# RWKV preparation of a hybrid encoder block: gate tiles between its projections, low-rank products of 128 rows

## The chip, the cores and the metric

One core of one Trainium2 chip. The metric is the device time of one execution in microseconds (us). TensorE (PE) has a granted clock, which the profile shows as a share of full speed; its two levels are 1.2 and 2.4 GHz.

## The reference, cut to what matters

One encoder block on 1024 tokens of width 1024. All branches read one input projection:

```
h    = rms_norm(x)                      # 1024 x 1024
proj = h @ w_in                         # columns: q k v | r k v (512 each) w,a (64+64) g (128) | gates 2 x 1024
attn = windowed attention of q, k, v (128-token blocks, +-128 tokens, sink)
zr   = proj[rwkv columns], shifted: zr + mu * (0.5 * (left + right neighbour) - zr)
w    = w0 + tanh(wl) @ w2 ;  a = sigmoid(a0 + al @ a2)     # low rank, 64 -> 512, for 2 directions
rw   = two RWKV-7 scans (forward, backward) over the tokens, plus a bonus term, normed, times g
gates = sigmoid(proj[gate columns])
x    = x + (gates[0] * (attn @ w_up_attn) + gates[1] * (rw @ w_up_rwkv)) @ w_out
# then a squared-ReLU MLP and a gated per-layer embedding
```

## The kernel before, in words

All large products are of fp32 data split into a high and a low part, and each product is three: high x high, low x high, high x low. A projection tile is 128 output columns by 512 tokens (one half of the tokens): 8 pieces of the contraction x 3 = 24 products of 128x512 in one PSUM buffer. PSUM buffers of these tiles ("mm") are two. A weight tile of 128 columns is loaded in two parts (`load_w`, line 193): DMA on SP's queue, a cast to the high part on ACT (line 187), the low part as a difference on POOL (line 188). There are two buffers of it (tag "w").

The program is written down in one order, and a tile scheduler places each instruction on its engine: by that order and readiness in its own model of time. On the chip each engine goes through its queue in order. Stretches written with `tc.high_priority(offset=-LOW)` come last whenever anything else is ready. `mmo` and `after` pin an order.

The stages that the change touches:

*Preparation* (lines 476 to 687). The two low-rank inputs z12 and z13 come first. Then for each of four pairs of heads p: the projections kz, rz and vz (two halves, 48 products each), each put through `shifted` (line 510): ACT copies the tile to "zr" (one buffer) and a scaled copy to "z", POOL adds the two neighbours ("sm"), DVE combines. vz's products are written with two hooks: after 8 of them the bonus sums of the pair before (`add_bonus`: rk split in two, products with a matrix of ones, line 569 and 570, eight transposes to "vt", line 583) and the split of this pair's squares, after 23 the norm sums. Then for both directions two low-rank products (`lora`, line 541): per half one product of 128 rows (line 547: high weights, high and low input above each other) and one of 64 rows (line 548: low weights, high input). ACT, DVE and POOL work the results into ra, bk, kd, rk, which go to DRAM. The buffer tag "gth" (two) is shared by the gates' outputs and by the second half's splits.

*Gate tiles* (`gates`, line 280): 16 tiles of columns m for each half h, tanh of the tile to DRAM. Half 0 is written as the generator `gates0`: 152 of its 384 products (`F0`) stand between p=3's low-rank products, the other 232 and the first two tiles of half 1 (48 products) stand behind the attention loop at the lowest priority, so that they fill in where PE has nothing else. The other 14 tiles of half 1 run beside the scan (`beside`), as before and after the change.

*Attention* (lines 805 to 882): 8 blocks n of 128 tokens; for both kv heads scores (line 839), row maximum on DVE, exponentials on ACT, transposes (line 860), products with V (line 868). In block 3 the scan's first low products are added, in block 5 the first inverse, 62 small DVE steps (line 749 and 752).

*Scan* (from line 1144): begins with `load_step` (line 1040: bkc, rac, UV) and `products` (line 1027, "gps", whose results are written where half 0 of the normed input lay).

The load of kT from DRAM (line 463) is issued on POOL's queue right behind the q/k/v stage, whose last transposes write kT_d.

## Time and profile before

| what | value |
|---|---|
| median of 3 runs | 1830.6 us (1830.04 to 1831.61) |
| profiled execution | 1829.44 us, span of its instructions 1827.7 us |
| PE busy | 1718.2 us (94% of the span), 11288 products |
| DVE, ACT, POOL busy | 1132.3, 879.1, 320.2 us |
| mean granted clock of PE | 0.977 |

"Busy" of PE is a sum over products whose ends are modelled and that overlap, so a busy PE is not one at its peak. A row of a timeline has the start, the duration, engine, line, operation, output<-input, shapes, count, and in brackets how long the engine stood idle before it and what released it.

### The profile page before, as it was taken

How to read it: one execution, taken by the hardware profiler on the slowest of the kernel's cores; microseconds unless marked ns; L12 is line 12 of the kernel's file. 1: busy time of each engine (PE TensorE's matmuls, PEld its weight loads, DVE VectorE, ACT ScalarE, POOL GpSimd, SP SyncE). 2: the span in 40 equal slices, each digit the busy share in tenths (PEclk: the TensorE clock that was granted, in tenths of full speed). 3: DMA queues.
4: the chain of work that ended last, by engine and by line, in shares of the span. 5: the costliest groups of instructions: out<-in, count | busy, mean ns of one | idle time of the engine just before them, and what ended most of it. 6: DMA issues, size and time to landing. Idle time of an engine off the chain costs nothing. (4 is left out here: it accounts for less than half of the span.)

```text
span 1827.7 us, 29641 instructions
## 1 busy us (share of the span) xinstructions
PE 1718.2 (94%) x11288; PEld 1376.0 (75%) x11288; DVE 1132.3 (62%) x1931; ACT 879.1 (48%) x1624; POOL 320.2 (18%) x265
## 2 busy tenths in 40 slices
PE   7999888999999898988889989999999999999998
PEld 7976666666677777766668867787887888888887
DVE  5646777745935656676464387666665877685442
ACT  5536666547754555456532255444444444554321
POOL 3454544532132121112132000000000000000000
PEclk9999999989999999999899989999999999999999
DMA  6362444674377474576565305544445974574111
GB/s 202 99 176 73 124 144 144 196 204 115 102 202 202 141 196 139 170 208 199 178 211 175 104 35 162 171 146 133 158 154 208 318 251 127 190 219 136 61 41 46
DMA packets 281998, 285.96 MB, mean 156 GB/s; under 512 B 49408, under 2 KB 195712, under 8 KB 281728
## 3 DMA queue, kind: packets, MB, share of 16 engines
q1 hardware_dynamic: 273600, 270.76, 48.1%
q0 software_dynamic: 7824, 12.59, 2.5%
q8 instruction: 89, 1.46, 0.3%
q10 hardware_dynamic: 432, 0.73, 0.1%
q14 instruction: 53, 0.43, 0.1%
HBM read 203.26 MB, written 80.74 MB: 155 GB/s over the span
## 5 line engine op out<-in xcount | busy, mean ns | idle before, releaser
L188 POOL TENSOR_TENSOR wlo<-wst,whi 128x512 fp32r<-128x512 f32 x100 | 149.5, 1507 | 318.7 <-ACT whi L187 263.3
L1688 PE MATMUL ff2ps<-th,sh 128*128 128x512 f32 x448 | 173.7, 390 | 2.9 <-ACT th L187 2.9
L1688 PE MATMUL ff2ps<-tl,sh 128*128 128x512 f32 x448 | 174.3, 389 | 0.0
L1688 PE MATMUL ff2ps<-th,sl 128*128 128x512 f32 x448 | 174.3, 389 | 0.0
L175 POOL TENSOR_TENSOR rstd<-ms,neghalf 128x1 f32<-128x1 f32 x24 | 13.2, 553 | 803.4 <-DVE ms L173 803.4
L187 ACT CAST sh<-sst 128x512 fp32r<-128x512 f32 x109 | 67.8, 622 | 116.3 <-PE ff2ps L1688 71.7
L188 DVE TENSOR_TENSOR sl<-sst,sh 128x512 fp32r<-128x512 f32 x109 | 75.1, 689 | 54.1 <-ACT sh L187 53.7
L1688 PEld LDWEIGHTS ff2ps<-th,sh 128*128 128x128 f32 x448 | 83.9, 188 | 21.1 <-ACT th L187 3.6
L1688 PEld LDWEIGHTS ff2ps<-tl,sh 128*128 128x128 f32 x448 | 84.1, 188 | 17.5 <-DVE tl L188 0.2
L1688 PEld LDWEIGHTS ff2ps<-th,sl 128*128 128x128 f32 x448 | 84.1, 188 | 17.5
L187 ACT CAST whi<-wst 128x512 fp32r<-128x512 f32 x100 | 60.7, 618 | 51.1 <-DMA wst<-in_w_in_dram 17.7
L187 ACT CAST w1h<-w1st 128x512 fp32r<-128x512 f32 x48 | 29.1, 614 | 104.4 <-DMA w1st<-in_w_ff_dram 102.9
L188 DVE TENSOR_TENSOR w1l<-w1st,w1h 128x512 fp32r<-128x512 f32 x48 | 32.7, 687 | 57.3 <-ACT w1h L187 57.3
L208 PE MATMUL gps<-rm,bkp 128*128 128x256 f32 x256 | 62.4, 386 | 1.5 <-DVE Z L752 1.0
L1034 DVE TENSOR_TENSOR gm<-gps,gmask 128x512 f32<-128x512 f32 x64 | 43.7, 685 | 29.9 <-PE gps L208 29.9
L218 PE MATMUL gmm<-hh,wlo 128*128 128x512 f32 x144 | 58.9, 409 | 0.0
L216 PE MATMUL gmm<-hl,whi 128*128 128x512 f32 x144 | 58.9, 409 | 0.0
L214 PE MATMUL gmm<-hh,whi 128*128 128x512 f32 x144 | 58.8, 408 | 0.0
L187 ACT CAST w1h<-ssum 128x512 fp32r<-128x512 f32 x64 | 39.4, 615 | 35.9 <-DVE ssum L1324 23.8
L208 PEld LDWEIGHTS gps<-rm,bkp 128*128 128x128 f32 x256 | 47.5, 190 | 11.0 <-issue 1.5
L1086 DVE COPY Wt<-wps 64x512 f32<-64x512 f32 x16 | 10.9, 679 | 71.5 <-PE wps L208 71.5
L226 PE MATMUL mm<-hh,whi 128*128 128x512 f32 x128 | 51.4, 401 | 4.0 <-ACT z L520 4.0
(409 smaller groups left out, 5058.0 us busy)
## 6 DMA issues: line engine op xcount, KB each, us to landing
wst<-in_w_in_dram SPq DMA_DIRECT2D x92, 256.0 KB, 3.5
tst<-in_w_ff_dram SPq DMA_DIRECT2D x80, 256.0 KB, 3.9
w1st<-in_w_ff_dram SPq DMA_DIRECT2D x32, 512.0 KB, 5.5
hid_S<-h SPq DMA_DIRECT2D x64, 256.0 KB, 2.1
sst<-hid_S SPq DMA_DIRECT2D x64, 256.0 KB, 2.7
hid_A<-h SPq DMA_DIRECT2D x48, 256.0 KB, 2.0
sst<-hid_A SPq DMA_DIRECT2D x45, 256.0 KB, 3.7
ra_d<-ra SPq DMA_DIRECT2D x8, 1024.0 KB, 4.5
```

The costliest lines, as they stand in the source:

```text
L175: nc.gpsimd.tensor_tensor(out=r, in0=ms, in1=neghalf.broadcast_to([P, width]), op=ALU.pow)
L187: a = nc.scalar.copy(hi, src)
L188: b = (lo_eng or nc.vector).tensor_tensor(out=lo, in0=src, in1=hi.bitcast(F32), op=ALU.subtract)
L208: tc.keep_in_program_order(nc.tensor.matmul(*a, **kw))
L214: mm(ps, ah, bh, start=(i == 0), stop=False)
L216: mm(ps, ah, bl, start=False, stop=False)
L218: mm(ps, al, bh, start=False, stop=(i == n - 1))
L226: nc.tensor.matmul(ps, ah, bh, start=(i == 0), stop=False)
L1034: nc.vector.tensor_tensor(out=gm[d][:, s % NB, 4 * h:4 * h + 4, :], in0=ps.rearrange("p j q t -> p (j q) t"), in1=gmask[:, d, :].unsqueeze ...
L1086: nc.vector.tensor_copy(Wt[own[0], 0], wp[own[0]])
L1688: nc.tensor.matmul(banks[bs][i], x_[:, isl], y_, start=fresh and p + j == 0, stop=p == NPR - 1 and j == 2, skip_group_check=True)
```

## The change

- `gates` takes a list of halves and uses one weight load for them. Tiles 0 and 1 are made for both halves in the preparation: tile 0 half 0 between kz and rz of p=0, tile 0 half 1 behind rz of p=0, tile 1 half 0 behind rz of p=1, tile 1 half 1 behind rz of p=2.
- `gates0` is then tiles 2 to 15 of half 0 (336 products): 152 in p=3 as before, 152 at the lowest priority, now written ahead of the attention loop, and 32 (`GTAIL`, 8 and 24) in block 7, each pinned behind the last score product of its kv head.
- The low part of the low-rank weights gets a tile of its own for each input, with zeros (written by ACT) in the other 64 rows, so that its product is of 128 rows.
- kT's load is issued in p=1 behind rz's "sm".
- rk shares the one buffer of vt and bv.

```diff
+GBOTH = ((1, 1), (0, 1), (0, 1), (0, 0))
+GTAIL = (8, 24)
-    def gates(h, ms=range(2 * KT), mm=nc.tensor.matmul):
+    def gates(halves, ms=range(2 * KT), mm=nc.tensor.matmul):
         for m in ms:
             c0 = O_GATE + m * P
             hi, lo = load_w(PW, "w", w_in[:, :, c0:c0 + P], P, parts=2)
-            ps = PMM.tile([P, 512], F32, name="gmm", tag="mm", bufs=2)
...
+            for h in halves:
+                ps = PMM.tile([P, 512], F32, name="gmm", tag="mm", bufs=2)
...
     kT = PY.tile([P, 2, 2, T], F32R, name="kT", tag="yk")
-    nc.gpsimd.dma_start(kT, kT_d)
...
-        wlr_l = A1.tile([P, ND, 512], F32R, name="wlrl")
+        wlr_l = [A1.tile([P, ND, 512], F32R, name=f"wlrl{i}") for i in range(2)]
...
-            nc.vector.tensor_tensor(out=wlr_l[hrows[i]], in0=st[hrows[i]], in1=wlr_h[i][hrows[i]].bitcast(F32), op=ALU.subtract)
+            nc.scalar.activation(out=wlr_l[i][lrows[i]], in_=st[lrows[i]], func=AF.Copy, scale=0.0)
+            nc.vector.tensor_tensor(out=wlr_l[i][hrows[i]], in0=st[hrows[i]], in1=wlr_h[i][hrows[i]].bitcast(F32), op=ALU.subtract)
...
-            nc.gpsimd.tensor_tensor(out=sm, in0=zr[:, 0:T], in1=zr[:, 2:T + 2], op=ALU.add)
+            last_sm[0] = nc.gpsimd.tensor_tensor(out=sm, in0=zr[:, 0:T], in1=zr[:, 2:T + 2], op=ALU.add)
...
-                nc.tensor.matmul(ps, wlr_l[hrows[i], d, cs_], lr[i][hrows[i], hs], start=False, stop=True)
+                nc.tensor.matmul(ps, wlr_l[i][:, d, cs_], lr[i][:, hs], start=False, stop=True)
...
-        gates0 = gates(0)
+        gates_both = gates((0, 1), range(GATT))
+        hold = [None]
+        def mm_held(*a, **kw):
+            i_ = nc.tensor.matmul(*a, **kw)
+            if hold[0] is not None:
+                after(i_, hold[0])
+        gates0 = gates((0,), range(GATT, 2 * KT), mm_held)
+        def gate_tiles(n):
+            for _ in range(n * 3 * KT):
+                next(gates_both)
...
             kz = shifted(O_RWKV + 512 + p * P, 4 + p)
+            gate_tiles(GBOTH[p][0])
             rz = shifted(O_RWKV + p * P, p, pin=p > 0)
+            gate_tiles(GBOTH[p][1])
+            if p == 1:
+                after(nc.gpsimd.dma_start(kT, kT_d), last_sm[0])
...
-                    rk = A1.tile([P, T], F32, name="rk", bufs=1)
+                    rk = A1.tile([P, T], F32, name="rk", tag="vt", bufs=1)
...
+        with tc.high_priority(offset=-LOW):
+            for _ in range((2 * KT - GATT) * 3 * KT - sum(F0) - sum(GTAIL)):
+                next(gates0)
         for n in range(NT):
...
-                        nc.tensor.matmul(sc, qT[:, 4 * kv + h, :], kT[:, kv, j, k0 * P:k1 * P], start=(j == 0), stop=(j == 1))
+                        held_behind = nc.tensor.matmul(sc, qT[:, 4 * kv + h, :], kT[:, kv, j, k0 * P:k1 * P], start=(j == 0), stop=(j == 1))
...
+                if n == NT - 1:
+                    hold[0] = held_behind
+                    for _ in range(GTAIL[kv]):
+                        next(gates0)
...
-        with tc.high_priority(offset=-LOW):
-            for _ in gates0:
-                pass
-            for _ in gates(1, range(GATT)):
-                pass
+        assert next(gates0, None) is None
...
-        yield from gates(1, range(GATT, 2 * KT), mmo)
+        yield from gates((1,), range(GATT, 2 * KT), mmo)
```

## Rows read from the trace of the kernel before

**Rows 1.** Stretches: start:end and length, busy us of each engine, granted clock, DMA.

```profile
124.60:164.80 40.20, 36.22 (x149) 28.78 (x148) 21.72 (x25) 20.17 (x29) 16.42 (x11) 0.96 0.35 115
164.80:215.40 50.60, 45.66 (x177) 33.77 (x177) 37.59 (x38) 32.12 (x45) 23.16 (x11) 0.93 0.45 135
...
317.40:366.00 48.60, 45.72 (x185) 33.50 (x184) 35.02 (x22) 27.96 (x42) 28.56 (x17) 0.98 0.62 185
...
383.70:462.40 78.70, 74.60 (x465) 48.69 (x465) 46.60 (x167) 56.99 (x157) 14.17 (x15) 0.98 0.53 142
462.40:510.70 48.30, 46.28 (x220) 28.76 (x220) 45.84 (x154) 34.46 (x93) 9.18 (x7) 1.00 0.31 88
510.70:522.00 11.30, 11.30 (x51) 9.34 (x51) 2.92 (x2) 7.03 (x9) 9.75 (x11) 1.00 0.75 216
```

**Rows 2.** Timeline of PE at the low-rank products of p=0.

```profile
164.62 0.39 PE L218 MATMUL mm<-hh,wlo 128*128 128x512 f32 x1
164.84 0.40 PE L547 MATMUL px<-lr,wlrh 128*128 128x512 f32 x1
165.17 0.50 PE L548 MATMUL px<-lr,wlrl 64*128 64x512 f32 x1
165.60 0.50 PE L547 MATMUL px<-lr,wlrh 128*128 128x512 f32 x1
```

**Rows 3.** Groups by line on PE, 120 to 383.7 us: busy us, mean ns, idle before.

```profile
L548 PE MATMUL px<-lr,wlrl 64*128 64x512 f32 x32 | 15.9, 498 | 0.0
```

**Rows 4.** Timeline of POOL before p=0.

```profile
127.82 0.56 POOL L463 DMA_DIRECT2D kT<-kT_d  x1 [8.69 <-DMA kT_d<-qkT]
128.39 1.91 POOL L522 TENSOR_TENSOR sm<-zr 128x1024 f32<-128x1024 f32 x1
```

**Rows 5.** Timeline of PE: first products of rz's two halves in p=0.

```profile
137.52 0.50 PE L226 MATMUL mm<-hh,whi 128*128 128x512 f32 x1 [1.70 <-ACT z L520]
...
145.68 0.50 PE L226 MATMUL mm<-hh,whi 128*128 128x512 f32 x1 [2.28 <-ACT z L520]
```

**Rows 6.** Timeline of PE at the border of p=0 and p=1: bonus and norm sums.

```profile
200.50 0.66 PE L569 MATMUL px<-s,one_r 128*128 128x512 f32 x1 [3.54 <-ACT s L187]
202.56 0.79 PE L570 MATMUL px<-s,one_r 128*128 128x512 f32 x1 [1.40 <-DVE s L188]
...
209.33 0.39 PE L569 MATMUL px<-s,one_r 128*128 128x512 f32 x1
```

**Rows 7.** Timelines of ACT and POOL in p=1.

```profile
198.31 1.15 ACT L623 ACTIVATE sq<-z,pc 128x1024 f32<-128x1024 f32 x1 [8.50 <-DVE z L523]
...
200.87 0.69 ACT L520 ACTIVATE z<-mm,omm 128x512 f32<-128x512 f32 x1
...
215.45 0.62 ACT L187 CAST whi<-wst 128x512 fp32r<-128x512 f32 x1 [0.17 <-PE mm L216]
...
221.08 3.11 POOL L188 TENSOR_TENSOR wlo<-wst,whi 128x512 fp32r<-128x512 f32 x1 [1.51 <-ACT whi L187]
```

**Rows 8.** Timeline of ACT: a pass over 64 rows.

```profile
133.91 1.06 ACT L531 ACTIVATE z<-z 64x1024 f32<-64x1024 f32 x1 [1.92 <-DVE zr L514]
```

**Rows 9.** Stretches of the gate products alone: PE, weight load, ACT, granted clock, DMA.

```profile
383.70:462.40 78.70, 29.38 (x91) 16.26 (x91) 1.76 (x3) 0.98 0.53 142
462.40:510.70 48.30, 22.42 (x74) 12.77 (x74) 1.76 (x3) 1.00 0.31 88
510.70:522.00 11.30, 11.29 (x49) 9.12 (x49) 1.20 (x2) 1.00 0.75 216
```

**Rows 10.** SP's queue: the scan's first load; its transfers' times to landing.

```profile
514.95 0.37 SPq L1046 DMA_DIRECT2D bkc<-bk_d  x1
...
DMA to landing us min/median/max: 2.7/4.3/6.9
```

**Rows 11.** Timeline of PE: first product and first transposes of the scan.

```profile
521.96 1.24 PE L208 MATMUL gps<-rm,bkp 128*128 128x256 f32 x5
...
527.27 1.03 PE L1059 MATMUL tmps<-ident,bkc 128*128 128x128 f32 x8
```

More of the change, by code (lines that the diff above doesn't have):

```diff
@@ L284, in gates @@
             hi, lo = load_w(PW, "w", w_in[:, :, c0:c0 + P], P, parts=2)
-            ps = PMM.tile([P, 512], F32, name="gmm", tag="mm", bufs=2)
-            yield from mm3_steps(ps, [(hi[:, k, :], lo[:, k, :], Hh[h][:, k, :], Hl[h][:, k, :]) for k in range(KT)], mm)
-            th = PW.tile([P, 512], F32, name="gth", tag="gth", bufs=2)
-            nc.scalar.activation(out=th, in_=ps, func=AF.Tanh, scale=0.5)
-            nc.sync.dma_start(g_d[m, :, 512 * h:512 * h + 512], th)
-            yield
+            for h in halves:
+                ps = PMM.tile([P, 512], F32, name="gmm", tag="mm", bufs=2)
+                yield from mm3_steps(ps, [(hi[:, k, :], lo[:, k, :], Hh[h][:, k, :], Hl[h][:, k, :]) for k in range(KT)], mm)
+                th = PW.tile([P, 512], F32, name="gth", tag="gth", bufs=2)
+                nc.scalar.activation(out=th, in_=ps, func=AF.Tanh, scale=0.5)
+                nc.sync.dma_start(g_d[m, :, 512 * h:512 * h + 512], th)
+                yield
     QW = pool(sQ, "wqkv")
@@ L505, in block_kernel @@
             nc.vector.tensor_copy(wlr_h[i], st)
-            nc.vector.tensor_tensor(out=wlr_l[hrows[i]], in0=st[hrows[i]], in1=wlr_h[i][hrows[i]].bitcast(F32), op=ALU.subtract)
+            nc.scalar.activation(out=wlr_l[i][lrows[i]], in_=st[lrows[i]], func=AF.Copy, scale=0.0)
+            nc.vector.tensor_tensor(out=wlr_l[i][hrows[i]], in0=st[hrows[i]], in1=wlr_h[i][hrows[i]].bitcast(F32), op=ALU.subtract)
         scan = A1.tile([P, T], F32, name="scan")
         nc.sync.dma_start(scan, I["scan"])
+        last_sm = [None]
         def shifted(c0, mi, pss=None, pin=False):
```

## The prediction

> **What bounds the kernel now.** I read the table of stretches first [rows 1]. Its stretches are the RWKV preparation (pair p=0; p=1, which stands for p=2 too; p=3), the attention's blocks 0 to 4 and 5 to 7, and the time between the attention's last product and the scan's first. PE is 94 to 100% busy from p=3 on; in the first two its busy sum is 36.2 of 40.2 us and 45.7 of 50.6 us at granted clocks of 0.96 and 0.93 (means over the two levels, 1.2 and 2.4 GHz). So behind p=2 what PE does comes nearest to setting the time, and in p=0 to p=2 something else does. The timelines say what. In p=0, PE waits 1.70 and 2.28 us for ACT to empty a PSUM buffer [rows 5]. ACT is late because POOL is: the load of kT stands first in POOL's queue, waits 8.69 us there for kT_d to land, and the first neighbour sum "sm" runs only at 128.39 [rows 4]; the next "zr" waits for that sum (one buffer). At the border from p=0 to p=1, PE is through with its projections and stands 3.54 and 1.40 us for the bonus sums [rows 6], which hang on DVE's chain (37.6 us busy of 50.6). It comes back at the lower level of the clock: 0.93 of 50.6 us is 3.5 us lost.
>
> Then I asked where the gate products run [rows 9]: 91 beside blocks 0 to 4, 74 beside blocks 5 to 7, and 49 in the 11.3 us behind the attention, beside nothing that the scan waits for.
>
> **The change, part by part.** A product in a run starts 0.23 us after the one before (164.62 to 164.84 [rows 2]).
>
> *Gate tiles in the preparation.* 96 gate products (2 tiles x 2 halves x 24) move from the attention to p=0 (48), p=1 (24) and p=2 (24).
> p=0: 48 x 0.233 = +11.2 us on PE. They cover the waits of 1.70 and 2.28 us and, with them, the lost clock (40.2 x 0.04 = 1.6 us): -5.6. PE has no other slack here before the norm sums, on which all of DVE's chain waits: +5.6. If only half of the waits goes, +8; if POOL's earlier start lets more of the chain run ahead, +3.
> p=1: the tile (24 x 0.233 = 5.6 us) fits into the stand of 4.9 us. The next projection, vz, needs the PSUM buffer that ACT frees at 200.87 + 0.69 = 201.6 (its "z" is queued behind "sq", which waits 8.50 us for DVE) [rows 7]. From there, 24 products and 4 sums at the full clock, 6.5 us, put the norm sums at 208.1 instead of 209.33 [rows 6]: -1.2. Bounds: -3.5 (all the clock loss) and +2.
> p=2: the same -1.2, but gate weights are now held: tile m=1 is loaded in p=1 and used again in p=2, and there are two weight buffers, so vz of p=1, k and r of p=2 share the other one. A buffer's refill begins when its last product is done (ACT cast at 215.45, released by PE [rows 7]) and is complete when POOL's second half ends, 221.08 + 3.11 = 224.2 [rows 7]: 8.7 us. Behind vz PE has the eight low-rank pairs (3.7 us at 0.46 each), behind k the gate tile itself (5.6 us), which can go first since its weights are there. Left open: 5.0 + 3.1 = 8 us, against 4.9 us of stand, the low-rank time saved below (3.2 us) and 3.5 us of clock. I take 0; bounds -3.5 and +12.
>
> *Low-rank products of all 128 rows.* Before, the step into and out of the 64-row product is 0.33 and 0.43 us, in pairs 0.43 each [rows 2]: 0.86 a pair, against 2 x 0.23 = 0.46. There are 32 [rows 3]: 12.8 us of PE time. In p=0 to p=2 (24 pairs, 9.6 us) PE has finished early anyhow; it pays for p=2's stall above, if at all. In p=3 gate products stand between the pairs and PE sets the pace: 8 x 0.40 = 3.2; DVE's chain there is 35.0 of 48.6 us busy, so I take -2.5 (bounds 0 and -12.8). The Trainium skill ("TensorE: Matmul & The Clock Gate", Part 2, and the table under "Why this matters for your kernels") says that a weight load takes its time by columns and that rows don't matter, and that a single product of few rows takes the time of a full one: by it, this edit would save 0 and the forecast be 2.5 us higher. The trace disagrees: 0.43 against 0.23. The rows decide.
> The zeros that fill the other 64 rows are two ACT passes of 64x1024 (one took 1.06 us [rows 8]) at the start, where ACT is busy 20.2 of 40.2 us [rows 1]; without that cover, +2.
>
> *kT's load* moves behind p=1's sum "sm": what waited behind it on POOL (sm, then ACT, then PE) is priced in p=0. In its new place its source landed long ago: its 0.56 us of issue [rows 4] delays a weight split that has slack. The attention needs it only at 383.7. 0.
> *rk in the buffer of vt/bv:* vt now waits until rk's split is done, and bv behind it; the norm sums come later than that. 0; without that cover, +1 in each of three pairs.
> *One weight load for both halves* of two tiles: four casts and four POOL splits fewer, hidden. 0.
>
> *The attention.* Behind p=3's fill 280 products are left before and 184 after. Before, 280 - 214 = 66 ran ahead of the first score [rows 9]; if so again, 118 are left, 32 of them held for block 7 (28 ran in its stretch before): 86 for blocks 0 to 6, and blocks 0 to 4 took 91. So blocks 0 to 4 stay as they are and 5 and 6 lose theirs (46). There DVE, which also does the inverse, is 45.8 of 48.3 us busy [rows 1]: little to gain, I take -1. Bounds: -10.7 (46 x 0.233, if PE sets that pace) and +4 (their own products, (46.3 - 22.4) / 3 = 8 us a block, take 16 at the lower level, as long as a block lasts now, 48.3 / 3, so that their waits would come on top).
> The Trainium skill (same page, "HAM oscillation") warns that idle stretches between groups of products bring the clock down; by that rule the +4 would be likely. The traces show both: full clock after 1.70 us of idle, the lower level after 2.28 [rows 5].
>
> *Behind the attention:* the 49 products leave, 11.3 us. Next late is the scan's load: bkc is issued at 514.95 and lands a median 4.3 us later [rows 10], so at 519.3, or at about 517 if the two weight loads ahead of it on SP's queue go elsewhere; its transposes came 5.3 us behind the scan's first product, 521.96 to 527.27 [rows 11], and would be due at 516 to 517 now. 0.3 to 2.5 us come back: -9 (bounds -11.3 and -6).
>
> Sum: +5.6 - 1.2 + 0 - 2.5 - 1 - 9 = **-8.1 us**. The profiled execution took 1829.44 us (span 1827.7 and 1.7 around it), so 1821.3; the median of the runs is 1.2 above it, so 1822.5. I say **1822**.
>
> **Rivals.**
> *The pinned weight buffer decides (slower).* Place: p=2. If the gate tile isn't taken ahead of r, the second refill stands whole: 5.0 + 8.7 us, and two returns at the lower clock (half of one border's loss, 1.75, each): 17 us less 4.9 of stand = 12: 1834. From 8 us on nothing of the gain is left. For it: 8.7 us [rows 7]. Against it: the scheduler orders by readiness, and the lower-clock part is there already before. 12%.
> *The attention was PE-bound throughout.* PE is 96% busy in blocks 5 to 7 too; all 46 products pay, 10 us more: 1812. Against it DVE's 95%. 13%.
> *The end isn't freed.* POOL's memsets, the scan's loads and ACT's copies of the inverse end as before, or the scheduler puts other gate products there, so that the change doesn't do what it says: 2 us instead of 9: 1829, no change. 13%.
> *My sum:* 62%, own range 1816 to 1827.
>
> 0.2% (3.7 us) is about what a measurement of this kernel can tell from no change. Below 1826.9 lie the PE-bound case and nearly all of mine, 74%; within 0.2%, the third rival and the edge of mine, 14%; slower 12%. The range 1810 to 1832 takes in the second and third rival and leaves out most of the slower one and the lowest ends.
>
> **What would show it.** Right: the POOL wait of 8.69 us and PE's 1.70 and 2.28 are gone; vz of p=0 starts some 5 us later; second products of a low-rank pair start 0.23 us after the first; the stand at 200 shrinks to 1 or 2 us and the granted clock of p=1 rises; no run of gate products stands between the last "po" and the first "gps", which follow within 2 us. Wrong: waits of k or r of p=2 for "wlo", blocks 5 and 6 clearly shorter, or the scan's first product as late as before.

## The result, and the profile after

The changed kernel takes 1836.7 us (median of 11 executions) against 1831.75 us of the kernel before on the same chip: ratio 1.0034, interval 1.0019 to 1.0048 (ratio and interval come from all executions of both; the two medians alone differ by 4.95 us). By the ratio that is 6.2 us slower (0.0034 x 1831.75) where 8.1 us less was forecast. The profiled execution took 1841.42 us with a span of 1839.6; it lies 4.7 us above its median and that of before 2.3 us below the median given here, so the two spans (+11.9 us) exaggerate. Up to the scan's first "ups" product, behind which the change touches nothing, the two traces differ by 5.7 us (549.9 before, 555.6 after), which agrees with the ratio; all differences below are taken up to there.

The stretches of the kernel after, cut at PE's norm sums (p=0 up to the norm sums, then up to those of p=1, of p=2 and of p=3, p=3 up to the first score, the attention up to the scan's first product): start:end, length, busy us of PE, PE weight load, DVE, ACT, POOL, granted clock, DMA. [rows 1] is cut some 6 us later, at the first low-rank product; at the norm sums the kernel before is cut at 158.7, 209.3, 260.2 and 311.3. In p=1 of the kernel after the two halves' sums lie 6 us apart (210.70 and 216.92), and the cut is at the second.

```profile
124.60:162.10 37.50, 37.50 (x164) 30.51 (x163) 17.20 (x17) 15.95 (x26) 16.05 (x11) 1.00 0.26 79
162.10:216.90 54.80, 48.43 (x203) 37.94 (x202) 40.55 (x38) 32.34 (x46) 23.85 (x12) 0.97 0.52 162
216.90:274.10 57.20, 48.24 (x199) 38.37 (x198) 37.38 (x36) 33.46 (x48) 23.48 (x13) 0.91 0.42 127
274.10:328.50 54.40, 44.59 (x178) 34.57 (x177) 39.38 (x38) 31.99 (x46) 23.11 (x11) 0.91 0.42 129
328.50:401.80 73.30, 64.45 (x275) 49.97 (x273) 37.58 (x28) 37.72 (x55) 41.14 (x27) 0.99 0.64 196
401.80:526.30 124.50, 113.97 (x639) 71.59 (x639) 94.10 (x320) 88.66 (x244) 20.41 (x20) 0.98 0.42 115
```

p=0 and the last row went the way that was forecast. The second to the fourth row take 54.8, 57.2 and 54.4 us; before, the stretches between the norm sums took 50.6, 50.9 and 51.1.

**What a pair is made of.** Two events cut a pair better than the norm sums do: ACT's square of kz ("sq"), and the last "ri" (DVE reads the second half's norm sum). From "ri" to the next pair's "sq" the kernel before takes 38.3, 38.3 and 38.3 us, the one after 38.4, 39.0 and 39.8: the chain through DVE, which the low-rank products feed and which is under 37.8 us in no run here. From "sq" to "ri" the kernel before takes 12.3, 12.6 and 12.7 us, the one after 16.2, 20.6 and 12.4. Most of the loss is there. Rows of PE at the border of p=0 and p=1, beside [rows 6]; first the kernel before, where vz's first products and the bonus's transposes go ahead of the stand, then the kernel after:

```profile
193.83 0.40 PE L214 MATMUL mm<-hh,whi 128*128 128x512 f32 x1
...
195.93 1.04 PE L583 MATMUL vtp<-ident,z 128*128 128x128 f32 x8
```

```profile
201.22 0.39 PE L221 MATMUL gmm<-hh,wlo 128*128 128x512 f32 x1
205.47 0.50 PE L217 MATMUL mm<-hh,whi 128*128 128x512 f32 x1 [3.86 <-ACT whi L190]
...
210.70 0.49 PE L576 MATMUL px<-s,one_r 128*128 128x512 f32 x1 [0.88 <-ACT s L190]
...
216.92 0.40 PE L576 MATMUL px<-s2h,one_r 128*128 128x512 f32 x1
217.35 0.50 PE L577 MATMUL px<-s2l,one_r 128*128 128x512 f32 x1
```

The gate tile ends at 201.6, and PE stands there for 3.86 us again, now for the weights of vz. Why they are late stands on ACT's queue (beside [rows 7]):

```profile
201.67 1.15 ACT L647 ACTIVATE sq<-z,pc 128x1024 f32<-128x1024 f32 x1 [8.52 <-DVE z L530]
...
204.23 0.69 ACT L527 ACTIVATE z<-mm,omm 128x512 f32<-128x512 f32 x1
204.81 1.13 ACT L190 CAST whi<-wst 128x512 fp32r<-128x512 f32 x2
...
209.06 1.07 ACT L591 COPY vt<-vtp 128x512 f32<-128x512 f32 x2 [3.12 <-DVE s2l L191]
```

vz's weights could be loaded only when r's last product had left their buffer, and by then ACT stood in "sq", waiting 8.52 us for DVE; the casts come five instructions behind it. The Trainium skill ("PSUM — Partial Sum Buffer", "Engine vs sequencer instructions") says that ScalarE's, VectorE's and GpSimdE's queues are strict FIFO; the row agrees: 204.81 for a cast that needs nothing of "sq". In the kernel before, vz's first nine products (193.83 to 195.70) were done ahead of the stand; their weights had been cast at 187.06.

DVE is late beside it. Its "bv" takes vt's buffer, and waits for vt's transfer to v_d, which runs beside kT's 2 MB. That transfer also starts late (210.16): the transposes to vt stood behind PE's wait, and ACT's copy to "vt" waits 3.12 us for DVE's split of rk, which now shares vt's buffer (last row above).

```profile
215.41 1.29 DVE L595 TENSOR_TENSOR bv<-px,z 128x512 f32<-128x512 f32 x2 [2.74 <-DMA v_d<-vt]
216.61 0.68 DVE L191 TENSOR_TENSOR s2l<-sq,s2h 128x512 fp32r<-128x512 f32 x1
```

In p=2 the gate tile is not taken ahead of rz. PE is through with kz and the bonus's transposes at 238.7, waits 7.30 and 1.62 us for rz's weights, and comes back at the lower clock level (0.63 us a product):

```profile
246.03 0.79 PE L229 MATMUL mm<-hh,whi 128*128 128x512 f32 x1 [7.30 <-ACT whi L190]
246.62 0.63 PE L230 MATMUL mm<-hl,whi 128*128 128x512 f32 x1
248.87 0.80 PE L231 MATMUL mm<-hh,wlo 128*128 128x512 f32 x1 [1.62 <-POOL wlo L191]
...
261.92 0.39 PE L217 MATMUL gmm<-hh,whi 128*128 128x512 f32 x1
...
276.92 0.50 PE L577 MATMUL px<-s2l,one_r 128*128 128x512 f32 x1 [1.91 <-DVE s2l L191]
```

The gate tile follows behind rz (261.92), and vz behind it, so the norm sums begin 17.2 us behind "sq" (274.13 and 256.90); in the kernel before it is 11 us.

On ACT the casts come behind a wait for DVE and seven instructions, most of them of the low-rank chain:

```profile
239.97 1.26 ACT L556 ACTIVATE th<-px,hb 128x512 f32<-128x512 f32 x2 [2.62 <-DVE bk L697]
...
245.37 1.13 ACT L190 CAST whi<-wst 128x512 fp32r<-128x512 f32 x2
```

And DVE's second split of p=2 waits until the gate tile's "gth", whose buffer tag it shares, has gone to DRAM; PE's last norm sum waits 1.91 us for that split (last row above):

```profile
276.17 0.69 DVE L191 TENSOR_TENSOR s2l<-sq,s2h 128x512 fp32r<-128x512 f32 x1 [3.50 <-DMA g_d<-gth]
```

The end is freed, and gives a little back (beside [rows 11]): the scan's first product follows the last "po" at once, and the next ones wait 1.43 us for "gm" and 1.29 us for bkc.

```profile
524.43 1.90 PE L899 MATMUL po<-pT,V 128*64 128x512 f32 x6 [0.85 <-DVE pT L893]
526.26 1.99 PE L211 MATMUL gps<-rm,bkp 128*128 128x256 f32 x8
...
530.61 1.99 PE L211 MATMUL gps<-rm,bkp 128*128 128x256 f32 x8 [1.43 <-DVE gm L1061]
...
535.26 0.63 PE L1086 MATMUL tmps<-ident,bkc 128*128 128x128 f32 x4 [1.29 <-DMA bkc<-bk_d]
```

The balance, by "ri" of each pair (before 160.0, 210.6, 261.5, 312.5; after 163.3, 217.9, 277.5, 329.7), first score, scan's first product, first "ups":

| stretch | before | after | difference | forecast |
|---|---|---|---|---|
| up to "ri" of p=0 | 160.0 | 163.3 | +3.3 | +5.6 |
| to "ri" of p=1 | 50.6 | 54.6 | +4.0 | -1.2 |
| to "ri" of p=2 | 50.9 | 59.6 | +8.7 | 0 |
| to "ri" of p=3 | 51.0 | 52.2 | +1.2 | none |
| to the first score | 71.2 | 72.1 | +0.9 | -2.5 |
| to the scan's first product | 138.3 | 124.5 | -13.8 | -10 |
| to the first "ups" | 27.9 | 29.3 | +1.4 | none |
| sum | | | +5.7 | -8.1 |

### The profile page after: what moved, and what is told of

It is laid out like the page before. It is cut to its first block, busy times and chain, and to the rows that moved or that the text cites. A ratio compares the mean times of both kernels' runs of the same rounds, so it can differ in the third digit from the quotient of the medians.

```text
span 1839.6 us, 29615 instructions
## 1 busy us (share of the span) xinstructions
PE 1708.2 (93%) x11288; PEld 1375.4 (75%) x11288; DVE 1139.8 (62%) x1931; ACT 878.4 (48%) x1622; POOL 315.2 (17%) x261
## 5 line engine op out<-in xcount | busy, mean ns | idle before, releaser
L191 POOL TENSOR_TENSOR wlo<-wst,whi 128x512 fp32r<-128x512 f32 x96 | 143.3, 1503 | 333.0 <-ACT whi L190 288.5
L178 POOL TENSOR_TENSOR rstd<-ms,neghalf 128x1 f32<-128x1 f32 x24 | 13.2, 552 | 806.5 <-DVE ms L176 806.5
L773 DVE TENSOR_TENSOR tmp<-Lp,Z 128x31 f32<-128x31 f32 (+15 forms) x124 | 52.7, 425 | 2.9 <-POOL Z L768 0.5
L1094 ACT ACTIVATE rac<-rac,Dt 128x128 f32<-128x128 f32 x120 | 38.8, 394 | 29.9 <-DMA rac<-ra_d 29.8
L231 PE MATMUL mm<-hh,wlo 128*128 128x512 f32 x128 | 51.4, 402 | 1.6 <-POOL wlo L191 1.6
```

The costliest lines, as they stand in the source:

```text
L191: b = (lo_eng or nc.vector).tensor_tensor(out=lo, in0=src, in1=hi.bitcast(F32), op=ALU.subtract)
L231: nc.tensor.matmul(ps, al, bh, start=False, stop=(i == n - 1))
L773: nc.vector.tensor_tensor(out=tv, in0=Lp[:, t + 1:32, t:t + 1].broadcast_to([P, n, m]), in1=Z[:, t:t + 1, 0:m].broadcast_to([P, n, m]), op ...
L1094: nc.scalar.activation(out=r_, in_=r_, func=AF.Copy, scale=Dt[:, d, j, s - 1:s])
```

## The experiments

Eighteen kernels; the ratio is to the kernel before on the same chip. The edits are shortened; "..." marks what is left out. In 15 of the 19 changed kernels of the table the first "ups" of the one profiled execution differs from that of before by what the ratio says, within 2.2 us; the other four are named where they come.

| kernel | "ri" to "sq" | "sq" to "ri" (p=1, 2, 3) | first score | first "ups" | ratio (interval) |
|---|---|---|---|---|---|
| before | 38.3 38.3 38.3 | 12.3 12.6 12.7 | 383.7 | 549.9 | 1 |
| after | 38.4 39.0 39.8 | 16.2 20.6 12.4 | 401.8 | 555.6 | 1.0034 (1.0019 to 1.0048) |
| own_load | 38.4 40.2 39.1 | 17.6 19.3 12.5 | 402.6 | 560.9 | 1.0054 (1.0035 to 1.0074) |
| p0_only | 38.3 37.9 38.0 | 16.3 13.8 13.6 | 389.3 | 551.0 | 1.0001 (0.9982 to 1.0020) |
| kt_later | 42.6 38.0 38.3 | 15.9 12.1 12.5 | 384.9 | 548.8 | 0.9987 (0.9971 to 1.0004) |
| rows128 | 38.8 38.5 38.5 | 13.7 13.2 14.2 | 386.4 | 550.0 | 1.0003 (0.9985 to 1.0021) |
| kt_vz | 39.6 42.6 42.6 | 11.4 11.7 11.8 | 383.5 | 549.1 | 0.9963 (0.9949 to 0.9977) |
| rk_in_vt | 39.7 38.8 38.7 | 13.3 13.0 13.9 | 386.6 | 551.6 | 1.0017 (0.9998 to 1.0037) |
| own_gth | 41.0 41.7 38.3 | 16.6 19.5 12.3 | 403.5 | 556.5 | 1.0048 (1.0029 to 1.0067) |
| rows64_own_rk | 42.5 39.8 44.2 | 17.9 21.3 12.9 | 415.0 | 573.2 | 1.0092 (1.0060 to 1.0124) |
| after_kt_vz | 38.4 38.0 39.9 | 16.2 22.7 12.2 | 404.8 | 560.8 | 1.0056 (1.0035 to 1.0077) |
| p0_kt_vz | 38.4 38.2 38.5 | 12.9 12.2 13.6 | 385.0 | 544.8 | 0.9980 (0.9962 to 0.9997) |
| rows128_kt_vz | 38.3 38.7 38.0 | 12.4 13.0 13.8 | 378.8 | 544.2 | 0.9979 (0.9962 to 0.9996) |
| between | 38.3 37.8 38.3 | 18.5 17.5 12.3 | 397.9 | 556.8 | 1.0026 (1.0008 to 1.0045) |
| r_weights | 38.4 38.0 38.0 | 17.0 14.7 12.9 | 395.5 | 550.9 | 1.0001 (0.9984 to 1.0017) |
| both_p1 | 38.4 38.3 38.6 | 23.7 13.4 13.0 | 404.0 | 558.7 | 1.0044 (1.0025 to 1.0063) |
| tail_only | 38.4 42.6 38.4 | 11.7 11.8 12.2 | 384.0 | 554.9 | 1.0033 (1.0015 to 1.0051) |
| gate_px | 38.4 38.8 38.0 | 16.4 15.6 13.6 | 396.9 | 548.4 | 0.9985 (0.9970 to 1.0000) |
| r_weights_px | 38.3 38.4 38.0 | 18.1 14.4 12.4 | 396.8 | 553.8 | 1.0001 (0.9987 to 1.0016) |
| kt_vz_px | 38.3 38.3 38.3 | 12.5 12.7 12.7 | 375.3 | 538.8 | 0.9972 (0.9952 to 0.9992) |

### The weights and the gate tiles' place

**own_load**: each gate tile loads its own weights, so that none stays in a buffer from p=1 to p=2.

```diff
-            hi, lo = load_w(PW, "w", ...)
             for h in halves:
+                hi, lo = load_w(PW, "w", ...)
```

> The changed kernel, but each gate tile loads its own weights, so that no weight buffer is held from one gate tile to the next. Theory 1 (a held weight buffer made PE wait in p=2): the waits of 7.30 us (for the cast) and 1.62 us (for the POOL split) in front of r in p=2 go, a wait of some 4 us in front of vz stays in p=1 and appears in p=2, where ACT is stuck behind the squares; p=2 some 4 to 6 us shorter, 1831 to 1834 us. Theory 2 (ACT's queue alone: any refill that comes behind the squares is late): same wait in p=1, p=2 about as long as now, 1836. Theory 3 (PE simply had no room for 24 products in a pair): no change, 1836 to 1838, since two loads are added.

Not faster: 1.0054, with an interval that overlaps the changed kernel's. In p=2 rz's waits of 7.30 and 1.62 us for its weights are gone, as theory 1 said; in their place rz waits 3.22 us for ACT's "z", vz 2.48 us for its own cast, and the norm sums 2.79 us for DVE's split, so p=2 is no shorter (40.2 + 19.3 us against 39.0 + 20.6). p=1 kept its wait (3.90 us). The pinned buffer alone is not the cause; to free it costs two loads more on ACT and POOL.

**p0_only**: gate tile 0 in p=0 stays, tile 1 of both halves goes beside the attention.

```diff
-GBOTH = ((1, 1), (0, 1), (0, 1), (0, 0))
+GBOTH = ((1, 1), (0, 0), (0, 0), (0, 0))
...
+            for _ in gates_both: pass    # lowest priority, ahead of the attention loop
```

> The changed kernel with gate tiles in p=0 alone (48 products); tile 1 of both halves (48) goes to the lowest priority ahead of the attention. Theory 1 and 2 (the borders of p=1 to p=3 lost time through buffers and queues): p=0 3 us later than before the change, p=1 and p=2 as long as before the change (50.6 and 50.9 us) or a little shorter, and what the attention gains shrinks by the 48 products that are back in it, of which it hides a part: 1822 to 1829 us. Theory 3 (no room in the preparation): p=0 costs all of 11 us, 1832 or more.

No change against before: the 0.33% to the changed kernel are the price of the tiles in p=1 and p=2, what they saved behind included. p=1 still has 16.3 us from "sq" to "ri": that is kT, below.

**between**: as own_load, the gate tiles of p=1 and p=2 between kz and rz.

```diff
-GBOTH = ((1, 1), (0, 1), (0, 1), (0, 0))
+GBOTH = ((1, 1), (1, 0), (1, 0), (0, 0))
```

> The changed kernel with the gate tile of p=1 and of p=2 between kz and rz instead of behind rz, each with a weight load of its own. If the loss of p=1 and p=2 is that a gate tile behind rz keeps vz's weight buffer (casts queued on ACT behind work that waits for DVE), then vz's weights come during rz here: the waits of 3.9 us (p=1) and 7.3 us (p=2) for the cast are gone, the pairs fall by 3 to 5 us each and the ratio to 0.999 or less. A wait of up to 3 us ahead of rz is to be expected (8.7 us of refill against 5.6 us of gate tile). If the loss is DVE's chain and the shared buffers (gth, vt), the pairs stay at 54 to 57 us and the ratio at 1.003 to 1.005.

A miss for both theories in size: vz's wait for the cast is gone in both pairs, but rz waits instead (2.05 us for the cast and 2.11 us for the low part in p=1), and "sq" to "ri" stays at 18.5 and 17.5 us. By the ratios it is 0.28% better than own_load; the intervals just overlap.

**r_weights**: tile 1's products take rz's weights, no load. Left out: tile 1's weight load, so its gate values are those of other columns.

```diff
-        hi, lo = load_w(PW, "w", ...)                      # in proj_steps
+        hi, lo = last_w[0] = load_w(PW, "w", ...)
...
+            own = m != 1 or len(halves) < 2
...
             for h in halves:
+                if not own:
+                    hi, lo = last_w[0]
```

> The changed kernel in which gate tile 1 (p=1 and p=2) loads no weights of its own: its products take rz's weights, which are there. Left out: tile 1's weight load, so its gate values are those of other columns; the count and shape of the products stay. Theory W (the loss in p=1 and p=2 is the wait for weights): vz's buffer is then kz's old one and is refilled during rz, so the waits of 3.86, 7.30 and 1.62 us are gone, each of the two pairs takes 51 to 53 us instead of 54.8 and 57.2, the first score comes at 392 to 395 instead of 401.8, and the ratio to before falls to 0.998 or less. Theory D (DVE's chain and the shared buffers set the pace, and PE would stand elsewhere): the pairs stay at 54 to 57 us with other waits, for the bonus or the norm sums, and the ratio at 1.002 to 1.004.

Between the two: 1.0001, 0.33% better than the changed kernel, where theory W asked for 0.998. The changed kernel's waits for weights are gone, p=2 has 14.7 us instead of 20.6; but p=1 has 17.0 us. Two waits stand where the weights' wait stood, PE's for the PSUM buffer that ACT's "z" frees and DVE's for v_d:

```profile
205.95 0.51 PE L217 MATMUL mm<-hh,whi 128*128 128x512 f32 x1 [3.35 <-ACT z L533]
```

```profile
217.20 1.29 DVE L601 TENSOR_TENSOR bv<-px,z 128x512 f32<-128x512 f32 x2 [4.54 <-DMA v_d<-vt]
```

**both_p1**: both halves of tile 1 in p=1.

```diff
-GBOTH = ((1, 1), (0, 1), (0, 1), (0, 0))
+GBOTH = ((1, 1), (0, 2), (0, 0), (0, 0))
```

> The changed kernel with both halves of gate tile 1 in p=1 (48 products behind rz), none in p=2. Theory W: one refill of the weight buffers (8.7 us) hides behind 11.2 us of gate products and the second is not needed, so p=2 takes 51 to 52 us, p=1 some 57, the first score comes 3 to 4 us earlier than 401.8, ratio 1.000 to 1.002. Theory D: p=1 takes 60 or more, and the ratio stays at 1.003.

Theory D's figures: p=1 has 23.7 us from "sq" to "ri", 11.4 more than before (48 products are 11.2), p=2 and p=3 are nearly as before. PE waits 3.37 us for "z" and 2.71 for "gth", both for a PSUM buffer.

**gate_px**: the gate tiles of the preparation in PSUM buffers of the small products (six) instead of the projections' two.

```diff
-                ps = PMM.tile(..., tag="mm", bufs=2)
+                ps = PX.tile(..., tag="px", bufs=6) if len(halves) == 2 else PMM.tile(..., tag="mm", bufs=2)
```

> The changed kernel with the gate tiles of the preparation in PSUM buffers of the small products (px, six) instead of the projections' two (mm). Theory P (two PSUM buffers hold PE back): vz's products need not wait for the gate tile's emptying and can go on while ACT's z is late; the pairs fall by 2 to 3 us each where the weights allow, first score 395 to 398 instead of 401.8, ratio 1.000 to 1.002. Theory W (weights alone): the waits for the casts stay and set the pace: pairs 54 to 57, ratio 1.003. Theory D (DVE's chain): the same ratio, with the waits moved to the bonus or norm sums.

0.9985, better than theory P's 1.000 and 0.49% under the changed kernel (by the ratios), with one line. p=1 is as it was (16.4 us, PE waits 3.90 us for the cast); p=2 falls from 20.6 to 15.6 and the way to p=3's "sq" from 39.8 to 38.0. In p=2 the gate tile now runs ahead of rz:

```profile
237.55 0.39 PE L231 MATMUL mm<-hh,wlo 128*128 128x512 f32 x1
237.78 0.39 PE L217 MATMUL gmm<-hh,whi 128*128 128x512 f32 x1
...
246.14 0.51 PE L229 MATMUL mm<-hh,whi 128*128 128x512 f32 x1 [2.99 <-ACT whi L190]
...
248.98 0.79 PE L231 MATMUL mm<-hh,wlo 128*128 128x512 f32 x1 [1.61 <-POOL wlo L191]
```

In the changed kernel it was not taken there although its weights lay ready: rz's two halves, written ahead of it, need both "mm" buffers, and its products stand behind rz's in PE's queue. One of the two was already empty when PE stopped at 238.7: ACT had emptied kz's first half at 236.3. The tag alone was changed, and with it the order; that the scheduler went by the buffers is the likely reason and is not shown. With the tile 24 us earlier its "gth" has long been stored, and the wait of 3.50 us for it is gone too.

**r_weights_px**: both edits.

> Gate tile 1 with rz's weights (its own load left out, so its gate values are those of other columns) and the preparation's gate tiles in px buffers. Theory W and P together: neither weights nor PSUM hold PE back, the waits of 3.35 and 3.53 us for ACT's z are gone, pairs of 50.5 to 52 us, first score 389 to 392, ratio 0.996 to 0.998. Theory D: PE waits at the bonus or norm sums instead, pairs 52 to 55, ratio 1.000 as with mm buffers.

Theory D's ratio, 1.0001, no better than r_weights: PE waits for DVE at p=1's bonus sums (2.36 us) and norm sums (2.10 us), and DVE's "bv" 5.88 us for v_d. Here one profile is 3.7 us worse than the ratio says.

### kT's load

**kt_later** and **kt_vz**: the kernel before with kT's load alone moved, behind the neighbour sum of p=1's rz, or of p=1's vz.

```diff
-    nc.gpsimd.dma_start(kT, kT_d)
...
             rz = shifted(...)                 # kt_later: here
+            if p == 1: after(nc.gpsimd.dma_start(kT, kT_d), last_sm[0])
             vz = shifted(...)                 # kt_vz: the same line behind this
```

> The kernel before with nothing but kT's load moved behind r's neighbour sum of p=1. If POOL's wait of 8.69 us was what made PE wait in p=0: PE's waits of 1.70 and 2.28 us and the lost clock go, 5 to 6 us less, 1825 to 1827 us against 1831. Rival (ACT and DVE work of z12 and z13 sets p=0's start, whatever POOL does): one of the two waits stays, 0 to 3 us less.

> The kernel before with kT's load moved behind the neighbour sum of vz in p=1, some 15 to 20 us later than where the change puts it. Theory (behind r's sum of p=1 the 2 MB transfer runs beside v_d's store, lands it in 9.8 us instead of 2.9 and makes DVE wait 6.86 us for it; this ate the 6.7 us that p=0 had gained): that wait goes, the norm sums of p=1 to p=3 stay 5 to 6 us earlier than before (311.3 to about 305), and the time is 1824 to 1826 us. Rival (the preparation's later pairs are paced by something that does not start with p=0): the norm sums of p=3 stand at 311 again, 1829 to 1831 us.

p=0 gains 6.8 us in kt_later ("ri" at 153.2 instead of 160.0), and p=1 gives 7.9 back (42.6 + 15.9 against 38.3 + 12.3); the ratio's interval holds no change. 4.3 of the 7.9 us lie between "ri" and "sq", ahead of the load (199.4), so they are not the load's: the granted clock is at the lower level from 163 to 173, from inside the low-rank products on (last section). The other 3.6 us lie at the border, where the transfers collide: kT's, issued at 199.4, makes vt's to v_d land after 9.8 us (7.5 is the longest before), and DVE waits for it. DVE's row, in kt_later:

```profile
209.89 1.29 DVE L589 TENSOR_TENSOR bv<-px,z 128x512 f32<-128x512 f32 x2 [6.86 <-DMA v_d<-vt]
```

The landing times of the transfers of v_d in the same kernel:

```profile
DMA to landing us min/median/max: 2.9/4.3/9.8
```

And the stretch of that wait, with a DMA share of 0.81 where the same 9 us of the kernel before (201 to 210) had 0.33:

```profile
199.00:208.00 9.00, 7.94 (x27) 6.40 (x28) 4.03 (x7) 4.95 (x10) 3.90 (x4) 0.73 0.81 259
```

The Trainium skill ("DMA: Bandwidth & Descriptors", "Issuing engines are not separate DMA queues") says that transfers issued by SP, ACT or GpSimd run on the same 16 engines and interleave; the rows agree, kT being on POOL's queue and v_d on SP's.

In kt_vz the collision is gone ("sq" to "ri" 11.4). The first score comes at 383.5, where it was, as the rival said, and yet the timed ratio is 0.9963, as the theory said; the profile (-0.8 us) and the ratio (-6.8 us) differ by 6.0 us, and what the profiled execution shows in p=2 and p=3 is told at the end.

**after_kt_vz**: the changed kernel with kT behind p=1's vz. **p0_kt_vz**: p0_only with it.

> The changed kernel with one edit: kT's load is issued behind the neighbour sum of p=1's vz instead of rz's. Theory A (kT's 2 MB transfer beside the transposes' small transfer v_d is a real part of the loss): DVE's bv in p=1 no longer waits 2.74 us for v_d, the norm sums of p=2 start 2 to 3 us earlier than 274.1, and the time falls by about 2.5 us: ratio to before 1.002. Theory B (whatever is gained at a border before p=3 goes back, as in the kernel before with kT moved, where the next two pairs took 54.3 instead of 51 us at a granted clock of 0.84): the first score stays at about 401 us and the ratio at 1.0034.

> Gate tile 0 for both halves in p=0 only, the 128-row low-rank products, kT's load behind p=1's vz; tile 1 of both halves beside the attention. With kT behind rz this kernel took 1.0001 of before. Theory A: kT's place was worth 2.5 us of that (p=1's vz and the norm sums behind it come earlier), ratio 0.9985, and the end is free as in that kernel. Theory B: the gain at p=1 is given back in p=2 and p=3; ratio 1.000.

Two answers. In p0_kt_vz theory A holds: p=1's "sq" to "ri" falls from 16.3 to 12.9, the wait of DVE with it (first row p0_only, second p0_kt_vz), and the ratio from 1.0001 to 0.9980.

```profile
215.56 0.69 DVE L595 TENSOR_TENSOR bv<-px,z 128x512 f32<-128x512 f32 x1 [5.36 <-DMA v_d<-vt]
```

```profile
213.09 1.29 DVE L595 TENSOR_TENSOR bv<-px,z 128x512 f32<-128x512 f32 x2 [2.23 <-DMA v_d<-vt]
```

In the changed kernel neither holds: 1.0056. p=1 stays at 16.2 us: PE's wait for vz's cast (3.88 us) is there as well, and of DVE's 2.74 us for v_d 1.96 us stay without kT. Besides, POOL's order changed: the split of kz's weights of p=2 now stands behind the load's issue (0.62 us) and behind "ra", which waits 4.16 us for ACT, so that kz waits 5.69 us for its low part. So p=1 of the changed kernel seems to have two obstacles side by side, where taking one away brings nothing; with both away it was not run.

### The low-rank rows, rk, and gth

**rows128**: the kernel before with the 128-row products (and rk in vt's buffer, without which there is no room); **rk_in_vt**: the latter alone; **rows64_own_rk**: the changed kernel with 64 rows and rk's own buffer; **own_gth**: 64 rows, rk shared, the gates' outputs in buffers of their own; **rows128_kt_vz**: rows128 and kt_vz.

```diff
-                nc.tensor.matmul(ps, wlr_l[hrows[i], d, cs_], lr[i][hrows[i], hs], ...)
+                nc.tensor.matmul(ps, wlr_l[i][:, d, cs_], lr[i][:, hs], ...)     # rows128
-                    rk = A1.tile([P, T], F32, name="rk", bufs=1)
+                    rk = A1.tile([P, T], F32, name="rk", tag="vt", bufs=1)       # rk_in_vt
-                th = PW.tile(..., name="gth", tag="gth", bufs=2)
+                th = PW.tile(..., name="gth", tag="gt2", bufs=2)                 # own_gth
```

> The kernel before with nothing but the low-rank products of 128 rows (and rk in vt's buffer, which makes the room). If the 64-row products cost PE 12.8 us of which p=3's 3.2 lie on the path: steps of 0.23 us in place of 0.43, 2 to 4 us less, 1827 to 1829. Rival 1 (DVE's chain sets p=3 too): no change, 1831. Rival 2 (vt waits for rk's split and ACT stands still in front of it at each border): 1 us more in each of three borders, 1832 to 1834.

> The kernel before with nothing but rk in the buffer of vt and bv. If it is this that lengthened each pair in the run with low-rank products of 128 rows (52.0 us in place of 50.7): ACT waits some 3 us for rk's second split in front of vt at each border, pairs of 51.5 to 52 us, 1 to 4 us more in all. If it was the faster products (their results come in another order): pairs of 50.7 us, no change.

> The changed kernel with the low-rank products of 64 rows and rk in its own buffer, as before the change: gate tiles, kT and the attention as changed. If the 128 rows and the shared buffer are worth nothing together, as alone: pairs and total as in the changed kernel, 1835 to 1838 us. If the shared buffer costs a microsecond or more a border and the rows give nothing: 3 to 5 us less. If the rows paid here, where PE is short: 3 to 6 us more.

> The changed kernel with buffers of their own for the gates' outputs (low-rank products back to 64 rows, which makes the room). Theory (the second half of the squares' split waits for a gate output's store, 3.50 us in p=2): DVE's wait for the store of g_d goes, the norm sums' second half follows the first at once, p=2 to p=3 2 to 3 us shorter. The waits for weights (3.9 and 7.3 us) stay. Rival: the wait only moves to the next late thing on DVE (v_d's store), the pairs are as long as in the changed kernel.

> The kernel before with kT's load behind p=1's vz and the low-rank products of 128 rows, rk in vt's buffer. kT's load there alone gave 0.9963 but two pairs at a granted clock of 0.84, whose second low stretch begins inside the low-rank products (0.43 us each, not idle). If it is the slower low-rank products that the clock falls in, products at 0.23 us keep it: pairs of 51 to 52 us, first score at about 380, ratio 0.995. If the clock falls all the same, pairs stay at 54 and the ratio at 0.996 to 0.998.

The step of the 128-row product is as priced, 0.23 us (rows of the changed kernel, beside [rows 2]):

```profile
170.25 0.39 PE L555 MATMUL px<-lr,wlrl 128*128 128x512 f32 x1
170.47 0.39 PE L554 MATMUL px<-lr,wlrh 128*128 128x512 f32 x1
170.70 0.39 PE L555 MATMUL px<-lr,wlrl 128*128 128x512 f32 x1
```

What it is worth depends on the kernel. In the kernel before it is nothing (rows128 1.0003, first score 386.4; rk_in_vt, with 64 rows, 386.6). In the changed kernel going back to 64 rows and to rk's own buffer costs 0.58% (1.0092 against 1.0034), 10.6 us, more than the 3 to 6 us expected; its profile is 6.4 us worse than that ratio. That this is near the 12.8 us of PE time counted in the prediction is luck: of the 17.6 us to the first "ups" 9.3 lie between "ri" and "sq" (42.5, 39.8 and 44.2 us), and in the first and the third of these PE falls to the lower level inside the low-rank products, without a stand. Rows of PE in rows64_own_rk, the low-rank product with 0.51 us first and then with 0.80 us:

```profile
172.44 0.51 PE L553 MATMUL px<-lr,wlrh 128*128 128x512 f32 x1
...
174.26 0.80 PE L553 MATMUL px<-lr,wlrh 128*128 128x512 f32 x1
...
176.30 0.63 PE L230 MATMUL mm<-hl,whi 128*128 128x512 f32 x1
```

rk in vt's buffer costs up to 3 us (first score 386.6; the ratio's interval holds no change too). own_gth takes the 3.50 us wait for "gth" away ("ri" to "sq" of p=3 38.3), but its 64-row products cost more (41.0 and 41.7 us in the two pairs before, at the lower level again). rows128_kt_vz has the first theory's pairs (51.1 us) and first score (378.8) and the second's ratio, 0.9979.

### The end

**tail_only**: the kernel before with all gate products ahead of the attention loop and 32 pinned in block 7; nothing moves into the preparation.

```diff
+GBOTH = ((0, 0), (0, 0), (0, 0), (0, 0))
+GTAIL = (8, 24)
...
+        with tc.high_priority(offset=-LOW):      # ahead of the attention loop
+            for _ in gates_both: pass
+            for _ in range(... - sum(F0) - sum(GTAIL)): next(gates0)
```

> The kernel before with one part of the change: gate tiles 0 and 1 and the rest of half 0 all stand ahead of the attention loop at the lowest priority, 32 products pinned behind block 7's scores; nothing moves into the preparation, kT, rk and the low-rank products are as before. If PE sets the pace of the attention as a whole, the 48 products that stood in the 11.3 us behind it cost about as much among its blocks: first score to the scan's first product stays at 135 to 138 us and the ratio at 0.999 to 1.001. If there is slack beside the blocks for 48 more, the stretch falls to about 130 and the ratio to 0.996.

Slower by 0.33%, outside both ranges, though the stretch from the first score to the scan's first product is the second theory's, 129.9 us. The scan's first product comes 8 us earlier (513.9), but behind it 59 gate products run on to 530 (group rows of PE, 515.3 to 530.5):

```profile
L604 PE MATMUL gmm<-hl,whi 128*128 128x512 f32 x20 | 8.1, 406 | 0.0
L604 PE MATMUL gmm<-hh,wlo 128*128 128x512 f32 x20 | 7.8, 396 | 0.0
L604 PE MATMUL gmm<-hh,whi 128*128 128x512 f32 x19 | 7.6, 402 | 0.2 <-ACT gth L292 0.2
```

So the attention's blocks take no more gate products than they had (156 between first score and scan, before 165). In the runs here the end is freed where products leave for the preparation.

### A faster kernel

**kt_vz_px**: kt_vz with vz's two tiles in px buffers.

```diff
 def proj_with(c0, hooks):
-                ps = PMM.tile([P, 512], F32, name="mm", tag="mm", bufs=2)
+                ps = PX.tile([P, 512], F32, name="mm", tag="px", bufs=6)
```

> The kernel before with kT's load behind p=1's vz, and vz's two tiles in px buffers instead of mm. If two PSUM buffers hold PE back at the border of two pairs (vz's first product waits for ACT's z behind the stalled square), vz runs ahead, norm sums come 1 to 2 us earlier per pair, first score at 379 to 381 instead of 383.5, ratio 0.994 to 0.996. If the bonus sums' wait for DVE and ACT sets the border, nothing changes: ratio 0.996 to 0.997. If low-rank products now wait for a px buffer, it is slower: 0.998 or more.

0.9972, not to be told from kt_vz's 0.9963; both beat the two given kernels, kt_vz with the narrower interval. Its profile is the best of all (first "ups" at 538.8, 6.0 us better than the ratio says), but not for the reason expected: "sq" to "ri" is 1 us longer than in kt_vz, and the gain lies between "ri" and "sq" (38.3 in all pairs against 39.6, 42.6 and 42.6), where kt_vz's clock is at the lower level. All four kernels with kT behind p=1's vz and no gate tile in p=1 and p=2 lie at 0.996 to 0.998.

## Why the prediction was wrong, by its steps

*p=0, +5.6*: right in its parts. PE is busy in all of the 37.50 us at full clock, POOL's wait and PE's 1.70 and 2.28 us are gone. From kz's first product to the norm sums it takes 39.1 us instead of 34.1, +5.0. That +3.3 was measured is luck by 1.6 us: kz starts at 122.97 instead of 124.59, because the kernel before, in its profile, runs at the lower level of the clock at 108 to 112, ahead of all that the change touches.

*p=1, -1.2*: **failed**. The step said that the gate tile fits into PE's stand and that vz then needs only the PSUM buffer freed at 201.6. The stand isn't free time for any work: ahead of it stood vz's first nine products and the bonus's transposes, and with these done the norm sums came 11 us behind "sq". The gate tile takes their place, and vz's weights cannot be there behind it, since r's buffer comes free only at r's end and ACT casts behind "sq". The step looked for vz's PSUM buffer and not for its weights; the eight transposes (about 1 us) were not in its sum either. +4.0. kT's load, which the prediction priced at 0 in its new place, runs beside a second wait there (DVE's 2.74 us, of which 1.96 stay in after_kt_vz without the load); in p0_only, where PE's wait for weights is absent, it costs 3.4 us. The sum looked at when its source landed, not at what lands beside it.

*p=2, 0*: **failed, and it is the largest miss**, +8.7, of which 8.0 lie between "sq" and "ri". It rested on the gate tile being taken ahead of rz "since its weights are there". It wasn't, and the two refills stood open as the rival of the pinned weight buffer had it (place p=2, +12, 1834). The sign named for it, a wait of r of p=2 for "wlo", is there (1.62 us). The rival had the place and nearly the price, the measured 1836.7 is nearest to it; its reason was short, though: own_load shows that unpinning alone doesn't help, and gate_px, that with another PSUM tag the tile goes ahead and p=2's "sq" to "ri" is 5.0 us shorter (the 1.9 us of the next sentence among them). About 1.9 us of the +8.7 are a term that the prediction doesn't have: PE's last norm sum waits for DVE's split, which waited 3.50 us for the store of "gth".

*p=3, no term*: +1.2. "ri" to "sq" is 39.8 us: behind the stand that "gth" leaves at the end of p=2, PE runs at the lower level (granted clock 0.60 from 279 to 282). In own_gth the stand and this stretch are absent, and it is 38.3.

*Low-rank rows, -2.5*: the price of a step was right (0.23 us), the place where it pays was not. In p=3 it pays nothing: PE waits 0.5 to 1.5 us four times for the gate weights' parts and 4.84 us for qT before the first score. In the changed kernel as a whole it is worth 10.6 us (with rk's buffer, which was changed together with it), which the prediction had set to "if at all"; about half of that, by the profile, is the clock, which the term doesn't have, and not the steps that it counted.

*rk in vt's buffer, 0*: the cover was missing in part. rk_in_vt has 1.0, 0.4 and 1.2 us more from "sq" to "ri", near the +1 a pair named for that case.

*Attention and end, -10*: right, -13.8, of which 1.4 comes back at "gm" and bkc (forecast at 0.3 to 2.5, inside the -9). tail_only fits the reason named, that the products leave. The count was exact: 118 gate products run between first score and scan.

Beyond single terms: the forecast counted PE's idle time in a pair as room. The pair is DVE's chain of 38.3 us (at full clock) and a stretch of 12.5 us from "sq" to "ri" that PE's queue sets. Work that is queued ahead of vz lengthens the second, however long PE stood in the first. What stays open: p=1 with both obstacles taken away (r_weights with kT behind vz) was not tried, nor a third weight buffer, for which there is no room.

## What to carry to other kernels

Before work is put into an engine's idle stretch, ask which queued work it goes ahead of, and whether its weights, its PSUM buffer and its output buffer are other ones than those that the next critical product needs; here one changed buffer tag was worth 0.5%. When two waits end at nearly the same time, removing one can show nothing, and the trace names only the later. A transfer that is off the critical path still delays a small one beside it, if a buffer waits for the small one.

## What the runs showed of the hardware that was not expected

A low stretch of the clock without a stand. In kt_vz, p=2 and p=3 take 54.3 us at a granted clock of 0.84, with a second stretch at the lower level that begins inside the low-rank products (267 to 279 us), behind 16 us in which PE did not stand for 0.3 us. The same second stretch, beginning inside the low-rank products with no stand of 0.3 us in the 10 us before, is in the profiles of six of the eight kernels with 64-row products: kt_later (163 to 173), kt_vz, own_gth (172 to 179 and 230 to 240), rows64_own_rk (174 to 184 and 297 to 307), tail_only (218 to 229) and, short, rk_in_vt (167 to 170). In the twelve with 128 rows each low stretch of p=0 to p=3 follows a stand. One of 10 us makes "ri" to "sq" about 4.3 us longer (42.6 instead of 38.3). With 128-row products (rows128_kt_vz) or vz in px buffers (kt_vz_px) the same pairs hold 0.93. One row of each, in that order:

```profile
202.00:256.30 54.30, 49.71 (x178) 36.07 (x177) 37.77 (x37) 31.99 (x45) 24.45 (x12) 0.84 0.53 167
```

```profile
201.80:252.90 51.10, 42.61 (x177) 33.47 (x176) 38.97 (x37) 31.94 (x45) 23.07 (x12) 0.93 0.55 175
```

```profile
201.90:252.90 51.00, 45.91 (x178) 34.13 (x177) 37.67 (x37) 32.12 (x46) 23.69 (x12) 0.93 0.56 176
```

The kernel before and kt_vz_px run the same 64-row products at 0.93. The cause stays open, and so does whether every execution of kt_vz has that second stretch; if not, that is where its ratio and its profile part.

Executions of one kernel differ by their granted clock. The 12 of kt_vz_px go from a span of 1817.8 us at a mean clock of 0.980 to 1835.5 at 0.969. A difference of a few us between two profiles is therefore read from the stretch that was changed, not from the spans.
